# The FFN's causal convolution: three taps out of PSUM on ScalarE and two two-tile sums on VectorE, where one tap was on ScalarE and four were on VectorE

## The chip, the cores and the metric

The kernel runs on one core of a Trainium2 chip. The metric is the device time of one execution in microseconds. The engines spoken of are TensorE (PE; its weight loads are PEld), VectorE (DVE), ScalarE (ACT) and GpSimd (POOL). SyncE (SP) issues the weight loads. Data lies in SBUF, and products are summed in PSUM, in banks of 128 partitions x 512 fp32 numbers.

## What is computed

One layer of a decoder on 256 tokens of width 2048: RMSNorm, a combined input projection, a gated linear recurrence and a dilated attention, their merge, then a convolutional FFN and a last RMSNorm. The change is in the FFN alone:

```python
h = h + conv_ffn(rmsnorm(h, norm2_g), w_up, conv_w, conv_b, w_down)

def conv_ffn(u, w_up, conv_w, conv_b, w_down):
    hup = u @ w_up                               # 256 x 11264
    hc = causal depthwise conv of width 3 over the tokens (hup, conv_w) + conv_b
    a, b = hc[..., :5632], hc[..., 5632:]
    return (gelu(a) * b) @ w_down
```

Channel c of the convolution at token t is w0 x[t-2] + w1 x[t-1] + w2 x[t] + bias.

## The kernel before

All weights stream from memory as 301 units of 1 MB, each of 16 blocks of 128 x 128, through three raw buffers; SyncE issues the loads two units ahead (LOOKAHEAD). Every fp32 weight is split in two parts, a rounded one by ScalarE (L344, or L289 in two_parts) and the rest by VectorE (L345, L290), and a product takes three matmuls: L558 to L560 for the up projection, L498 to L500 for the others. The splits of a unit are written two units ahead of its matmuls, and there are six buffers for them in this stage. Every engine works through its own queue in order.

The FFN goes in 11 blocks b of 4 channel tiles for each of the two branches a and b. The up projection of a block (`sevenfold`) uses a seven-product scheme: units of a kind called S need sums of weight blocks first, made by VectorE (q at L312, raw at L314 to L317), then split as sa, se, sf and sg by L289 and L290. Its seven sums lie in seven PSUM banks; the eighth (`late_bank(8)`) belongs to the convolution.

What follows a block's up projection is the generator `hidden_side(b)`. It is advanced a step whenever a weight unit begins: `pump` gives it SIDE_US = 1.8 us a unit, and a `yield SIDE_US` spends as much, so that its instructions stand in the queues between the products of the next units. Its steps: `unfold` makes four tiles c out of the seven sums, with three accumulating DMAs by GpSimd (L582) from the scaled tiles e2, e4, e3; HIDDEN_WAIT = 3 empty steps; `convolve` for branch a (tile ua, PSUM tile ua..t), GELU over all of it (L1010); `convolve` for branch b (ub); the product g = a * g (L1016), and its split into two parts (ff) for the down projection.

`convolve` takes two halves i of two channel tiles c each. A half transposes its four 128 x 128 pieces into the one bank (L993). Then ScalarE writes the last tap and the bias of each tile (L996, Identity with a scale and a bias), and VectorE adds the other two taps, reading the bank again: L997 over 255 tokens, L998 over 254. The next half's transposes need the bank, so they wait for the last reader of this half. TensorE takes its instructions in the order of the program, so all its products behind them wait too.

After a block's up projection the down products of an earlier block follow (`DOWN`, tile dn). Each of their banks is copied by ScalarE into a staging tile dns (L1038) and added to h by an accumulating DMA of GpSimd (L1039). Staging tiles are 128 x 512; `stage` hands them out from five buffers in turn (tag o2), for unfold's t, v and e tiles and for dns. A buffer is free again when its last reader is done, which for e and dns is a DMA. The last block adds into h by VectorE (L1035).

Of the kernel before, what the change touches and what calls it, by code (L numbers as in the profile page):

```python
# [14 lines left out]
AF = mybir.ActivationFunctionType  # L15
ALU = mybir.AluOpType
# [3 lines left out]
T = 256  # L20
# [163 lines left out]
def hybrid_block(ctx, tc, x_p, x_t, weights, g1, gf, params, c_rope, c_mask0, c_mask1, c_level, out):  # L184
    nc = tc.nc
    vec, act, pe = nc.vector, nc.scalar, nc.tensor
# [13 lines left out]
    def w4(shape, name, dt=F32):  # L200
        return sb.tile([P] + list(shape), dt, tag="w4", name=name, bufs=22)

    def stage(name):
        return late["stage"].tile([P, 512], F32, tag="o2", name=name, bufs=5 if "pool" in late else STAGES - 2)
# [14 lines left out]
    def side_bank(name):  # L219
        turn[1] += 1  # L220
        return bank(4 + (turn[1] - 1) % 4, name)
# [13 lines left out]
    def pc(name, i=0):  # L235
        return par[:, POFF[name][0] + i : POFF[name][0] + i + 1]
# [419 lines left out]
    scale = float(P) ** -0.5  # L656
# [203 lines left out]
    for g in range(NGRP):  # L860
        z = four(f"z{g}", True)
        f = w4([2, HG, P], f"f{g}")
        act.activation(f, z, AF.Sigmoid)
        act.activation(z, z, AF.Sigmoid, scale=-1.0)
        for h in range(HG):
            i = g * HG + h
# [15 lines left out]
    for n in range(2):  # L882
        for j in range(NJ):
            t = w4([2, 512], f"eg{n}_{j}")
# [24 lines left out]
    for j in range(NJ):  # L909
# [7 lines left out]
        for m in range(2):  # L917
# [3 lines left out]
            pt = side_bank(f"mixt{j}_{m}")  # L921
            for c in range(4):
                pe.transpose(pt[:, c * P : (c + 1) * P], ya[:, c * P : (c + 1) * P], ident)
            pt = pt.rearrange("p (c t) -> p c t", c=4)
# [8 lines left out]
    for j in range(NJ):  # L933
        t = w4([2, 512], f"h{j}")
# [19 lines left out]
    for j in range(NJ):  # L954
# [4 lines left out]
        for i in range(2):  # L959
            pt = side_bank(f"ht{j}_{i}").rearrange("p (c t) -> p c t", c=2)  # L960
            for c in range(2):
                for m in range(2):
                    n = (2 * i + c) * P
# [15 lines left out]
    def late_bank(i, name):  # L979
        return bank(place[i], name)  # L980
# [4 lines left out]
    def convolve(ups, c0, t, name):  # L985


        for i in range(2):
            pt = late_bank(8, f"{name}t{i}").rearrange("p (c t) -> p c t", c=2)
            for c in range(2):  # L990
                for m in range(2):
                    n = (2 * i + c) * P
                    pe.transpose(pt[:, c, m * P : (m + 1) * P], ups[m][:, n : n + P], ident)  # L993
            for c in range(2):
                d, s, col = t[:, 2 * i + c], pt[:, c], c0 + 2 * i + c
                act.activation(d, s, AF.Identity, bias=pc("cb", col), scale=pc("cw2", col))  # L996
                vec.scalar_tensor_tensor(d[:, 1:], s[:, : T - 1], pc("cw1", col), d[:, 1:], op0=ALU.mult, op1=ALU.add)  # L997
                vec.scalar_tensor_tensor(d[:, 2:], s[:, : T - 2], pc("cw0", col), d[:, 2:], op0=ALU.mult, op1=ALU.add)  # L998
            yield SIDE_US

    ff = {}
# [1 line left out]
    def hidden_side(b, sums):  # L1003

        c11, c21, c12, c22 = unfold(sums, rstd2, neg2, f"up{b}")
        for _ in range(HIDDEN_WAIT - (b == 0)):
            yield SIDE_US
        a, g = (late["pool"].tile([P, FB, T], F32, tag="uc", name=f"u{n}{b}", bufs=2) for n in "ab")
        yield from convolve((c11, c21), b * FB, a, f"ua{b}")
        gelu = act.activation(a, a, AF.Gelu_apprx_tanh)  # L1010
        if b == NBLK - 1:

            with in_turn(gelu):
                act.activation(small([1], "tab", "tab", 1), eps, AF.Sqrt)
        yield from convolve((c12, c22), NFF + b * FB, g, f"ub{b}")
        vec.tensor_tensor(g, a, g, op=ALU.mult)  # L1016
        ff[b] = [w4([2, 2, T], f"ff{b}_{i}", F32R) for i in range(2)]
        for i in range(2):
            d, s = ff[b][i], g[:, 2 * i : 2 * i + 2]
            two_parts(d[:, :, 0], d[:, :, 1], s)  # L1020
# [5 lines left out]
    for b in range(NBLK):  # L1026
# [4 lines left out]
        for j, b0, b1 in DOWN.get(b, ()):  # L1031
            pst = moving(ff_parts, b0 * FB, (b1 - b0) * FB, f"dn{b}_{j}", [late_bank(i, f"dn{b}_{j}_{i}") for i in ((4, 3) if j % 2 else (1, 5))])
            for m in range(2):
                if b == NBLK - 1:
                    vec.tensor_tensor(ht[j][:, m], ht[j][:, m], pst[m], op=ALU.add)  # L1035
                else:
                    t = stage(f"dns{b}_{j}_{m}")
# [11 lines left out]
    for m in range(2):  # L1049
# [16 lines left out]
        v, r, t = v3[:, mc], r3[:, mc], s3[:, mc]  # L1066
# [57 lines left out]
```

## Time and profile before

| what | value |
|---|---|
| three runs | 1745.98, 1748.06 (median), 1751.34 us |
| profiled execution | 1748.59 us, of which the span is 1746.8 us |
| granted TensorE clock, mean | 0.997 |
| ScalarE, busy | 988.6 us, 57% |
| VectorE, busy | 1289.9 us, 74% |
| FFN stage | from about 1047 to 1738 us of the span |

The profile gives the time of each instruction in microseconds from the start of the span. A line of a timeline has the start, the duration, the engine, the line of the code, the operation, output<-inputs, the shapes and, in brackets, how long the engine sat idle before it and what ended that. Groups of instructions give the count, then the busy time in us and the mean duration in ns. Rows of waits give who waited for whom, the total, the count and the longest. The chain of waits follows the work that ended last back to what released it. Busy times of neighbours overlap a little, since an engine starts an instruction before the one before it is written out.

### The profile page before, as it was taken

Reading aid. Unit: us, or ns where it says so; the run is one execution under the profiler, and the core shown is the slowest. Engines: PE = TensorE matmul, PEld = TensorE weight load, DVE = VectorE, ACT = ScalarE, POOL = GpSimd, SP = SyncE. Lnnn points to the kernel's source line nnn. Section 1 sums busy time; section 2 is a strip of 40 time slices with the busy share of each in tenths; the row PEclk is TensorE's granted clock in tenths of the full one; section 3 lists DMA queues with packets and bytes.
Section 4 is the critical chain, followed back from the end, with each engine's and each line's share of the span. In section 5 each row is a group of like instructions: output and inputs, shape, how many; then the busy total and the mean of one; then the engine's idle time right before and its main releaser. Section 6 shows DMA issues by size and latency. Waiting matters only on the chain.

```text
span 1746.8 us, 21528 instructions
## 1 busy us (share of the span) xinstructions
PE 1726.3 (99%) x8352; PEld 1442.7 (83%) x8352; DVE 1289.9 (74%) x1610; ACT 988.6 (57%) x1253; POOL 70.1 (4%) x94
## 2 busy tenths in 40 slices
PE   9999999999999999999999999999999999999998
PEld 7888888888888888888888887788878888788886
DVE  7665575776858675444656679789988988888977
ACT  6444465555455555444445567676666666566663
POOL 0000000000000000000000000110010010010000
PEclk9999999999999999999999999999999999999999
DMA  7665644444444444556455556676677676676672
GB/s 277 230 208 199 230 145 145 170 167 172 166 169 169 169 170 168 193 193 241 178 186 190 188 189 216 194 232 228 200 235 238 190 237 235 190 235 231 198 259 97
DMA packets 58310, 346.13 MB, mean 198 GB/s; under 512 B 6704, under 2 KB 6960, under 8 KB 20064
## 3 DMA queue, kind: packets, MB, share of 16 engines
q1 hardware_dynamic: 45504, 318.02, 50.9%
q0 software_dynamic: 11408, 23.34, 6.7%
q10 hardware_dynamic: 1296, 3.41, 0.5%
q8 instruction: 65, 1.06, 0.2%
q14 instruction: 37, 0.30, 0.0%
HBM read 321.41 MB, written 2.10 MB: 185 GB/s over the span
## 4 chain that ended last, share of the span: by engine, by line
PE 90%; DMA 4%; DVE 3%; issue 1%; ACT 1%; SPq 0%; DVEq 0%; ACTq 0%
PE up L558 8%; PE up L559 8%; PE up L560 8%; DMA raw<-weights 4%; PE egp L500 3%; PE egp L498 3%; PE egp L499 3%; PE dn L498 3%; PE dn L500 3%; PE dn L499 3%; PE ak L411 3%; PE aq L411 2%; PE gp L498 2%; PE wo L498 2%; PE wo L500 2%; PE gp L500 2%
## 5 line engine op out<-in xcount | busy, mean ns | idle before, releaser
L345 DVE TENSOR_TENSOR hl<-raw,hl 128x1024 fp32r<-128x1024 f32 (+1 forms) x518 | 628.7, 1219 | 317.7 <-ACT hl L344 316.5
L344 ACT ACTIVATE hl<-raw 128x1024 fp32r<-128x1024 f32 (+1 forms) x518 | 543.2, 1054 | 536.8 <-PE egp L500 79.4
L498 PE MATMUL dn<-hl,ff 128*128 128x512 f32 x320 | 126.1, 394 | 0.0
L499 PE MATMUL dn<-hl,ff 128*128 128x512 f32 x320 | 124.8, 390 | 0.0
L500 PE MATMUL dn<-hl,ff 128*128 128x512 f32 x320 | 124.5, 390 | 0.0
L558 PE MATMUL up<-hl,hva 128*128 128x512 f32 x264 | 104.1, 394 | 0.0
L559 PE MATMUL up<-hl,hva 128*128 128x512 f32 x264 | 103.7, 393 | 0.0
L560 PE MATMUL up<-hl,hva 128*128 128x512 f32 x264 | 103.7, 393 | 0.0
L498 PE MATMUL egp<-hl,xu 128*128 128x512 f32 x256 | 100.5, 393 | 0.0
L500 PE MATMUL egp<-hl,xu 128*128 128x512 f32 x256 | 99.8, 390 | 0.0
L499 PE MATMUL egp<-hl,xu 128*128 128x512 f32 x256 | 99.7, 389 | 0.0
L500 PEld LDWEIGHTS dn<-hl,ff 128*128 128x128 f32 x320 | 60.1, 188 | 12.7
L498 PEld LDWEIGHTS dn<-hl,ff 128*128 128x128 f32 x320 | 60.1, 188 | 12.1
L499 PEld LDWEIGHTS dn<-hl,ff 128*128 128x128 f32 x320 | 60.1, 188 | 12.0
L411 PE MATMUL ak<-xu,hl 128*128 128x512 f32 x192 | 68.0, 399 | 0.0
L290 DVE TENSOR_TENSOR sa<-raw,sa 128x1024 fp32r<-128x1024 f32 x40 | 48.9, 1222 | 18.3 <-ACT sa L289 18.2
L558 PEld LDWEIGHTS up<-hl,hva 128*128 128x128 f32 x264 | 50.1, 190 | 10.7 <-ACT up0e L581 0.4
L560 PEld LDWEIGHTS up<-hl,hva 128*128 128x128 f32 x264 | 50.1, 190 | 10.5
L559 PEld LDWEIGHTS up<-hl,hva 128*128 128x128 f32 x264 | 50.1, 190 | 10.3
L500 PEld LDWEIGHTS egp<-hl,xu 128*128 128x128 f32 x256 | 48.0, 188 | 10.0
L289 ACT ACTIVATE sa<-raw 128x1024 fp32r<-128x1024 f32 x40 | 42.3, 1057 | 24.6 <-PE up L560 8.9
L499 PEld LDWEIGHTS egp<-hl,xu 128*128 128x128 f32 x256 | 48.1, 188 | 9.8
(575 smaller groups left out, 4198.7 us busy)
## 6 DMA issues: line engine op xcount, KB each, us to landing
raw<-weights SPq DMA_DIRECT2D x298, 1024.0 KB, 4.8
h<-dns POOLq DMA_DIRECT2D x36, 256.0 KB, 7.5
h<-x_t ACTq DMA_DIRECT2D x4, 512.0 KB, 5.1
xt<-x_p SPq DMA_DIRECT2D x3, 512.0 KB, 10.2
xs_q<-aqraw POOLq DMA_DIRECT2D x6, 256.0 KB, 6.9
xs_k<-akraw POOLq DMA_DIRECT2D x6, 256.0 KB, 7.2
raw<-weights SPq DMA_DIRECT2D x2, 512.0 KB, 6.6
gfb<-gf POOLq DMA_DIRECT2D x2, 512.0 KB, 13.6
```

What stands on the lines that cost most here:

```text
L289: act.activation(hi, src, AF.Copy)
L290: vec.tensor_tensor(lo, src, hi.bitcast(F32), op=ALU.subtract)
L344: last[0] = act.activation(hi[:, q * w : (q + 1) * w], raw, AF.Copy)
L345: last[1] = vec.tensor_tensor(lo[:, q * w : (q + 1) * w], raw, hi[:, q * w : (q + 1) * w].bitcast(F32), op=ALU.subtract)
L411: pe.matmul(ps, hi, pair, start=(k == 0), stop=False, skip_group_check=True)
L498: pe.matmul(pst[m], xl, hi, start=(k == k0), stop=False)
L499: pe.matmul(pst[m], xh, hi, start=False, stop=False)
L500: pe.matmul(pst[m], xh, lo, start=False, stop=(k == k0 + nk - 1))
L558: pe.matmul(sums[b], xl, wh, start=b in fresh, stop=False)
L559: pe.matmul(sums[b], xh, wh, start=False, stop=False)
L560: pe.matmul(sums[b], xh, wl, start=False, stop=left[b] == 0)
```

## The change

All three taps of a tile are now read out of the bank by ScalarE: the last one with the bias as before (Identity, now L999), and the two others with Copy and the weight as scale (L1001), into two staging tiles e, one for each tap, with room for both channel tiles of the half. VectorE then adds them from SBUF, in one tensor_tensor per tap over both tiles at once (L1003: 128x2x254 for w0's, 128x2x255 for w1's). The bank's readers are now ScalarE's alone. Each half needs two staging tiles that it didn't need before, out of the same five buffers.

```diff
@@ -991,11 +991,16 @@
                 for m in range(2):
                     n = (2 * i + c) * P
                     pe.transpose(pt[:, c, m * P : (m + 1) * P], ups[m][:, n : n + P], ident)
+
+            taps = [stage(f"{name}e{n}{i}").rearrange("p (c t) -> p c t", c=2) for n in range(2)]
+            d = t[:, 2 * i : 2 * i + 2]
             for c in range(2):
-                d, s, col = t[:, 2 * i + c], pt[:, c], c0 + 2 * i + c
-                act.activation(d, s, AF.Identity, bias=pc("cb", col), scale=pc("cw2", col))
-                vec.scalar_tensor_tensor(d[:, 1:], s[:, : T - 1], pc("cw1", col), d[:, 1:], op0=ALU.mult, op1=ALU.add)
-                vec.scalar_tensor_tensor(d[:, 2:], s[:, : T - 2], pc("cw0", col), d[:, 2:], op0=ALU.mult, op1=ALU.add)
+                col = c0 + 2 * i + c
+                act.activation(d[:, c], pt[:, c], AF.Identity, bias=pc("cb", col), scale=pc("cw2", col))
+                for n, e in enumerate(taps):
+                    act.activation(e[:, c], pt[:, c], AF.Copy, scale=pc(f"cw{n}", col))
+            for n, e in enumerate(taps):
+                vec.tensor_tensor(d[:, :, 2 - n :], d[:, :, 2 - n :], e[:, :, : T - 2 + n], op=ALU.add)
             yield SIDE_US
 
     ff = {}
```

Per half, ScalarE goes from 2 to 6 instructions and VectorE from 4 to 2. Over the program, VectorE's rows go from 1584 to 1496, ScalarE's from 1224 to 1400, and TensorE's stay at 7885. In the changed kernel, GELU is L1015, the product L1021 and the copy into dns L1043.

The order of work around the convolution moves too. VectorE in block 1, where the two halves of ua meet (ua1t0 and ua1t1 are their PSUM tiles, 190 the unit whose weights are summed in q). Before:

```order
L290 TENSOR_TENSOR se188_8483<-raw188_8437,se188_8483 128x1024
L997 SCALAR_TENSOR_TENSOR ua1_8495<-ua1t0_8497,par_85,ua1_8495 128x255
L312 TENSOR_TENSOR q190_8575<-raw190_8538 128x512
L998 SCALAR_TENSOR_TENSOR ua1_8495<-ua1t0_8497,par_85,ua1_8495 128x254
L314 TENSOR_TENSOR raw190_8538<-raw190_8538 128x512
L290 TENSOR_TENSOR sf188_8487<-raw188_8437,sf188_8487 128x1024
L997 SCALAR_TENSOR_TENSOR ua1_8495<-ua1t0_8497,par_85,ua1_8495 128x255
L998 SCALAR_TENSOR_TENSOR ua1_8495<-ua1t0_8497,par_85,ua1_8495 128x254
L345 TENSOR_TENSOR hl189_0_8532<-raw189_8493,hl189_0_8532 128x1024
L997 SCALAR_TENSOR_TENSOR ua1_8495<-ua1t1_8540,par_85,ua1_8495 128x255
L998 SCALAR_TENSOR_TENSOR ua1_8495<-ua1t1_8540,par_85,ua1_8495 128x254
```

and now (ua1e00 and ua1e10 are the staging tiles of w0's and w1's taps for half 0, ua1e01 and ua1e11 those of half 1):

```order
L290 TENSOR_TENSOR se188_8499<-raw188_8453,se188_8499 128x1024
L312 TENSOR_TENSOR q190_8599<-raw190_8558 128x512
L314 TENSOR_TENSOR raw190_8558<-raw190_8558 128x512
L1003 TENSOR_TENSOR ua1_8511<-ua1_8511,ua1e00_8518 128x2x254
L290 TENSOR_TENSOR sf188_8503<-raw188_8453,sf188_8503 128x1024
L1003 TENSOR_TENSOR ua1_8511<-ua1_8511,ua1e10_8519 128x2x255
L345 TENSOR_TENSOR hl189_0_8552<-raw189_8509,hl189_0_8552 128x1024
L1003 TENSOR_TENSOR ua1_8511<-ua1_8511,ua1e01_8565 128x2x254
L1003 TENSOR_TENSOR ua1_8511<-ua1_8511,ua1e11_8566 128x2x255
L345 TENSOR_TENSOR hl189_1_8555<-raw189_8509,hl189_1_8555 128x1024
```

Four taps out of PSUM around q and the split sf have become two sums out of SBUF, and all four sums of ua1 now stand behind q.

ScalarE in block 4, from the copies of the down products to the convolution of ub. Before:

```order
L1038 ACTIVATE dns4_3_1_9977<-dn4_3_3_9874 128x512
L289 ACTIVATE sa222_9989<-raw222_9937 128x1024
L1010 ACTIVATE ua4_9894<-ua4_9894 128x1024
L289 ACTIVATE se222_9994<-raw222_9937 128x1024
L996 ACTIVATE ub4_9895<-ub4t0_10007,par_85 128x256
L344 ACTIVATE hl223_0_10039<-raw223_10004 128x1024
L289 ACTIVATE sf222_9998<-raw222_9937 128x1024
L289 ACTIVATE sg222_10001<-q222_9987 128x512
L344 ACTIVATE hl223_1_10042<-raw223_10004 128x1024
L996 ACTIVATE ub4_9895<-ub4t0_10007,par_85 128x256
L289 ACTIVATE sa224_10084<-raw224_10045 128x1024
L289 ACTIVATE se224_10089<-raw224_10045 128x1024
```

and now:

```order
L1015 ACTIVATE ua4_9958<-ua4_9958 128x1024
L1043 ACTIVATE dns4_3_0_10046<-dn4_3_4_9937 128x512
L1043 ACTIVATE dns4_3_1_10049<-dn4_3_3_9938 128x512
L289 ACTIVATE sa222_10061<-raw222_10005 128x1024
L999 ACTIVATE ub4_9959<-ub4t0_10079,par_85 128x256
L289 ACTIVATE se222_10066<-raw222_10005 128x1024
L1001 ACTIVATE ub4e00_10084<-ub4t0_10079,par_85 128x256
L1001 ACTIVATE ub4e10_10085<-ub4t0_10079,par_85 128x256
L999 ACTIVATE ub4_9959<-ub4t0_10079,par_85 128x256
L1001 ACTIVATE ub4e00_10084<-ub4t0_10079,par_85 128x256
L1001 ACTIVATE ub4e10_10085<-ub4t0_10079,par_85 128x256
L344 ACTIVATE hl223_0_10115<-raw223_10076 128x1024
```

GELU stands ahead of the copies now, and all six taps of ub's first half stand ahead of the splits hl223_0 and sf222; the first tap is behind sa222, the others behind se222.

TensorE in block 4, at the transposes of ub's second half (ub4t1). Before:

```order
L560 MATMUL up5_2_9981<-sa222_9989,hvs2_7336 128x512
L558 MATMUL up5_7_9986<-se222_9994,hvx2_7337 128x512
L559 MATMUL up5_7_9986<-se222_9994,hvx2_7337 128x512
L993 MATMUL ub4t1_10047<-ident_87,up4c12_9784 128x128
L993 MATMUL ub4t1_10047<-ident_87,up4c22_9785 128x128
L993 MATMUL ub4t1_10047<-ident_87,up4c12_9784 128x128
```

and now:

```order
L558 MATMUL up5_5_10056<-sg220_9953,hvx0_7161 128x512
L559 MATMUL up5_5_10056<-sg220_9953,hvx0_7161 128x512
L560 MATMUL up5_5_10056<-sg220_9953,hvx0_7161 128x512
L993 MATMUL ub4t1_10123<-ident_87,up4c12_9848 128x128
L993 MATMUL ub4t1_10123<-ident_87,up4c22_9849 128x128
L993 MATMUL ub4t1_10123<-ident_87,up4c12_9848 128x128
```

They have moved from the last summed products of unit 222 ahead to those of unit 220. Between the transposes of ub's first half and these stood 49 matmuls, and now 21; from ua's first half to its second it was 30 and is 24, and from ua's second to ub's first 22 and is 24. The units and their loads stay in the same order.

## The prediction

> **What bounds the kernel now.** I read the page's head first, for who is busy.
>
> ```profile
> span 1746.8 us, 21528 instructions
> PE 1726.3 (99%) x8352; PEld 1442.7 (83%) x8352; DVE 1289.9 (74%) x1610; ACT 988.6 (57%) x1253; POOL 70.1 (4%) x94
> ```
>
> TensorE is busy for all but 20.5 us of the span. The change leaves its instructions alone, so a gain can only be idle time of TensorE, or work that it does at a low clock. The busy time that VectorE sheds and ScalarE takes on counts only through that. Second I read whom TensorE waits for; the columns are the total, the count and the longest, in us.
>
> ```profile
> PE ua1t L993 <- DVE ua L998: 3.4, 1, 3.4
> PE ua7t L993 <- DVE ua L998: 2.4, 1, 2.4
> PE ua0t L993 <- DMA up0c<-up0e: 1.2, 1, 1.2
> PE ua2t L993 <- DVE ua L998: 1.1, 1, 1.1
> PE ua4t L993 <- DVE ua L998: 0.7, 1, 0.7
> PE ua7t L993 <- DMA up7c<-up7e: 0.5, 1, 0.5
> PE ua9t L993 <- DVE ua L998: 0.2, 1, 0.2
> PE ub4t L993 <- DVE ua L998: 0.2, 1, 0.2
> ```
>
> The convolution's transposes (L993) wait for VectorE's last tap (L998): a half of a block can't be transposed into the single bank while the half before it is still being read. These rows make 3.4 + 2.4 + 1.1 + 0.7 + 0.2 + 0.2 = 8.0 us. The two DMA rows wait for the bank's input. Third, the chain through the longest of them (start, duration, what):
>
> ```profile
> 1107.20 8.40 DMA raw<-weights
> ...
> 1115.63 0.69 DVE q L312
> 1116.32 0.39 DVE ua L998
> 1116.72 0.60 DVE raw L314
> 1117.32 1.14 DVE sf L290
> ...
> 1118.88 0.49 DVE ua L998
> ...
> 1119.51 1.09 PE ua1t L993 x4
> ...
> 1124.43 0.43 PE up L558
> ```
>
> VectorE is not slow here. A weight DMA of 8.40 us lands late, the operand sum q (L312) waits for it, and the last taps stand behind q in VectorE's queue; TensorE stands behind the taps. Then the matmuls come every 0.43 us, in place of the 0.23 that the last row below shows, and the windows of the stall, the time after it and the time after that (us, then the busy time of PE, PEld, DVE, ACT and POOL, clock, DMA share, GB/s) say why:
>
> ```profile
> 1115.00:1119.50 4.50, 1.06 (x5) 0.58 (x4) 3.83 (x7) 1.51 (x2) 0.00 (x0) 0.87 0.53 88
> 1119.50:1125.10 5.60, 5.59 (x16) 4.54 (x17) 2.72 (x4) 2.07 (x3) 0.00 (x0) 0.50 0.47 178
> 1125.10:1130.00 4.90, 4.90 (x25) 4.07 (x24) 3.26 (x6) 3.05 (x4) 0.00 (x0) 1.00 0.53 214
> ```
>
> The granted clock is 0.50 for 5.6 us behind the stall. Eleven matmuls at 0.43 instead of 0.23 cost 2.2 us, and four transposes in 1.09 instead of the usual 0.63 us cost 0.5: the stall's true price is 3.4 + 2.7 us. The Trainium skill (TensorE: Matmul & The Clock Gate, Why this matters for your kernels) says that TensorE falls to half clock after an idle gap of over about 3 us; by that rule the 3.4 us stall pays twice, the 2.4 us one not, and the trace agrees: 0.50 behind the first, full pace behind the second, below.
>
> ```profile
> 1494.61 0.63 PE L993 MATMUL ua7t<-ident,up7c 128*128 128x128 f32 x4 [2.36 <-DVE ua L998]
> 1495.23 0.23 PE dn L498
> ```
>
> **VectorE's part.** Durations, of one L997, of the nearest two-tile sum (512 columns a row, from SBUF), and of the exact form of the new taps, a Copy of 128x256 out of PSUM with a pointer as scale, alone and as a pair:
>
> ```profile
> 1111.57 0.48 DVE L997 SCALAR_TENSOR_TENSOR ua<-ua1t,par,ua 128x255 f32<-128x255 f32 x1
> L290 DVE TENSOR_TENSOR ff<-ub,ff 128x512 fp32r<-128x512 f32 x22 | 14.2, 687 | 0.5 <-ACT ff L289 0.5
> L967 ACT ACTIVATE hg<-ht,par 128x256 f32<-128x256 f32 x16 | 6.7, 467 | 1.9 <-PE ht L964 1.9
> 942.82 0.84 ACT L967 ACTIVATE hg<-ht,par 128x256 f32<-128x256 f32 x2 [0.46 <-PE ht L964]
> ```
>
> There are 44 halves (11 blocks, two branches, two halves). VectorE goes per half from 4 x 0.48 = 1.92 us to 2 x 0.69 = 1.38, so it sheds 44 x 0.54 = 24 us. None of it is on the path by itself. What counts is that VectorE no longer reads the bank: all six L993 rows above that name it, 8.0 us, lose their cause, and with the long one goes the 2.7 us of low clock. I put -10.7 us, with 0 as the other end if something else is as late.
>
> **What is late next, in block 1.** The DMA that came late feeds q, and the first split of that unit (sa) comes much later:
>
> ```profile
> 1128.05 1.23 DVE L290 TENSOR_TENSOR sa<-raw,sa 128x1024 fp32r<-128x1024 f32 x1 [1.57 <-ACT sa L289]
> ```
>
> It starts 12.4 us after the landing at 1115.6 and waits for ScalarE. If TensorE runs 6.1 us earlier, 6.3 us are left, so the DMA is not next. But the adds (L1003) stand behind q as the taps did, and GELU behind the adds, and the next branch's taps behind GELU on ScalarE. From 1115.6, VectorE needs q, raw, an add, sf, an add, a split and two adds: 0.6 + 0.6 + 0.6 + 1.1 + 0.6 + 1.1 + 1.3 = 5.9, to 1121.5. GELU is then 1.05 us, six taps and two splits 4.4, to 1127. The transposes that wait for them are due at 1115.9 + 24 matmuls + 0.6 + 21 or 22 matmuls + 0.6 = 1127.5 or so. That is about even; I put +1.0 us here (0 to 2).
>
> **ScalarE's part.** Each half gains four L1001 of 0.47 us, 0.37 when they follow each other: 1.5 to 1.9 us, 66 to 82 us in all. The block is where that has to fit:
>
> ```profile
> 1288.00:1312.00 24.00, 23.08 (x108) 18.64 (x107) 19.85 (x28) 16.02 (x21) 3.53 (x4) 1.00 0.70 192
> 1301.60 0.23 PE dn L500
> 1301.18 1.28 ACT L1038 ACTIVATE dns<-dn 128x512 f32<-128x512 f32 x2 [0.19 <-PE dn L500]
> 1302.36 1.05 ACT L289 ACTIVATE sa<-raw 128x1024 fp32r<-128x1024 f32 x1
> 1303.31 1.05 ACT L1010 ACTIVATE ua<-ua 128x1024 f32<-128x1024 f32 x1
> 1302.97 0.63 PE L993 MATMUL ub4t<-ident,up4c 128*128 128x128 f32 x4 [0.23 <-DVE ua L998]
> 1314.59 0.61 PE L993 MATMUL ub4t<-ident,up4c 128*128 128x128 f32 x4
> ```
>
> ScalarE works 16.0 of these 24 us; four halves' new taps add 6 to 7.5, and it would work 22 to 23.5, that is 92 to 98%. And the second half of ub, now 11.6 us and 49 matmuls behind the first, moves to 21 matmuls behind it: 0.6 + 21 x 0.23 = 5.4 us. The order on ScalarE is then: two staging copies, sa, the first tap, se, five taps. Copies start 0.4 us before the last down matmul does (1301.60 less 1301.18, the chain's row and the copies') and give way to sa after 1.18 us; sa and se hold 0.95 each, the six taps some 0.40: done 5.1 us after that matmul's start. The transposes come 0.2 + 5.4 = 5.6 us after it. The margin is 0.4 to 0.5 us, for ua by the same count 0.8. A wait of 0 to 0.6 us for ub in each of the seven blocks 3 to 9 is what these hold; I take 0.2 x 7 = 1.4, since a negative margin takes a split more than the order has, and keep 0 and 4.2.
>
> The five staging buffers are taken by two taps a half too, so a tap waits until the accumulating DMA of an older dns has landed:
>
> ```profile
> DMA to landing us min/median/max: 3.3/7.5/11.0
> ```
>
> The third dns of a block must land for the last tap of ub's second half, some 7 us after its issue: about 1 us of hold at the median, 4 at the longest. Behind it in ScalarE's queue stand splits, whose lead decides whether that counts:
>
> ```profile
> 1283.00:1350.00 67.00, 66.08 (x300) 54.15 (x299) 59.40 (x75) 43.98 (x56) 6.14 (x7) 1.00 0.73 228
> 1299.48 1.06 ACT L344 ACTIVATE hl<-raw 128x1024 fp32r<-128x1024 f32 x1 [1.15 <-PE dn L500]
> 1462.95 1.23 DVE L290 TENSOR_TENSOR sf<-raw,sf 128x1024 fp32r<-128x1024 f32 x1
> 1465.70 0.39 PE L558 MATMUL up<-sf,hvx 128*128 128x512 f32 x1
> ```
>
> The first row is a whole block, windows as above: ScalarE is idle for 23 of 67 us. In the convolution's stretch it waits for TensorE to free the buffers of a split (1.15 us), so it has lead, and I price the hold at nothing. The cover is thinnest at the last summed unit of a block: split done at 1464.18, used at 1465.70, 1.5 us. The waits for c (1.2 + 0.5) stay.
>
> **Sum.** 1748.6 (span and 1.8 around it) - 8.0 - 2.7 + 1.0 + 1.4 = 1740.3. The profiled execution is 0.5 above the median of the runs: 1739.8, said as 1740.
>
> **Rivals.** *No measurable change, 0.27.* The waits change their owner. One more split (0.95) ahead of the taps than I count, and each of blocks 1 to 9 loses 0.55 at ub and 0.15 at ua: 6.3, with 2 in block 1: 1737.9 + 8.3 = 1746, less 0.5. For it: margins of 0.4 and 0.8 us and a nearly full ScalarE. Against: a split ahead of the taps is one less behind them, and only the place in the queue shifts.
>
> *Slower, 0.12.* ScalarE becomes the bound of each block: held by the staging slots and by 7.5 us more work per block (four halves of 1.9), it falls behind with the splits, past the 1.5 us of lead at the last summed unit. If 3.4 us of lag are left there, ten blocks lose 1.9 us each: 1737.9 + 19 = 1757. It decides from a lag of 1.5 us, and pays from 2.6 (ten times 1.07 eats the 10.7). Against it: of the block's 23 idle us, 15 would be left after the 7.5, and the last summed unit lies at the block's end, far behind the convolution. The Trainium skill (ScalarE: Activation LUTs, Rules for kernel authors) says to do adds and multiplications on VectorE, not on ScalarE. By that rule the taps' scaling is in the wrong place, and this rival is what it would cost; the trace bears it out only weakly, with 467 ns for a tap on ScalarE against 480 on VectorE.
>
> *The stall returns at another door, in the forecast's share.* If block 1 still stops TensorE for over 3 us, the 2.7 us stay too: 1740.3 + 2.7 + 2.4 = 1745, near the first rival. That the change doesn't free the bank from VectorE is excluded by its lines.
>
> **How the numbers follow.** A measurement of this kernel tells about 0.3%, 5.2 us, from no change: faster is below 1742.8, slower above 1753.3. The forecast has 0.61; the first rival 0.27, the second 0.12. The range reaches from 1736 (the floor of 1737.9 less the 2 us by which the lowest run lies under the median) to 1749, which takes in the first rival and the scatter of the runs, and leaves out the second. The signed chances are faster 0.6, same 0.28, slower 0.12, for the forecast's upper edge touches 1742.8.
>
> **What would show it.** Right: no L993 row that names VectorE, clock 1.00 from 1115 to 1125, VectorE about 24 us less busy, ScalarE 66 to 82 more, L993 waits for ScalarE of 1 to 4 us in all. Wrong: L993 waits for ScalarE of 6 us or more; matmuls (L498, L558) that wait for a split; a window at clock 0.50.

## The result and the profile after

The changed kernel takes 1740.04 us (median of five runs, 1737.84 to 1740.83), against 1748.06 us before. The ratio is 0.9947, with a 95% interval of 0.9929 to 0.9965: about 8 us faster. Its profiled execution took 1740.42 us, with a span of 1738.6.

The head of the page first:

```profile
span 1738.6 us, 21613 instructions
PE 1723.5 (99%) x8352; PEld 1442.6 (83%) x8352; DVE 1271.5 (73%) x1522; ACT 1045.4 (60%) x1429; POOL 70.1 (4%) x94
```

VectorE is 18.4 us less busy and ScalarE 56.8 us more. TensorE's busy time fell by 2.8 us although it does the same work. 1.0 of that lies ahead of block 0's transposes; of the rest, 1.1 is low clock, which cost 2.7 us behind the old stall and 1.6 behind the new one below. Whom TensorE waits for, all rows of the FFN stage (total, count, longest):

```profile
PE ub1t L993 <- ACT ub1e L1001: 2.3, 1, 2.3
PE ua0t L993 <- DMA up0c<-up0e: 1.6, 1, 1.6
...
PE ua2t L993 <- ACT ua2e L1001: 0.5, 1, 0.5
```

No transposes wait for VectorE any more: six rows and 8.0 us are gone. In their place stand two rows with ScalarE, 2.8 us. The same three windows around block 1's old stall, and one more (us, busy time of PE, PEld, DVE, ACT and POOL, clock, DMA share, GB/s):

```profile
1115.00:1119.50 4.50, 4.50 (x22) 3.67 (x21) 4.04 (x6) 3.73 (x8) 0.00 (x0) 1.00 0.20 36
1119.50:1125.10 5.60, 5.60 (x28) 4.64 (x27) 4.52 (x6) 3.36 (x6) 0.00 (x0) 1.00 0.75 236
1125.10:1130.00 4.90, 2.62 (x11) 1.89 (x11) 4.87 (x7) 4.90 (x9) 0.00 (x0) 0.87 0.38 159
...
1129.00:1131.00 2.00, 2.00 (x6) 1.51 (x6) 2.00 (x4) 2.00 (x6) 0.00 (x0) 0.50 0.35 57
```

The old stall and its half clock are gone. A new stall sits 8.5 us later (1128.05 for 1119.51), and the half clock stands behind that one. Its making, in one row each of VectorE, ScalarE and TensorE (start, duration, and in brackets the idle time before and what ended it):

```profile
1115.42 0.69 DVE L312 TENSOR_TENSOR q<-raw 128x512 f32<-128x512 f32 x1 [4.26 <-DMA raw<-weights]
1121.74 1.06 ACT L1015 ACTIVATE ua<-ua 128x1024 f32<-128x1024 f32 x1 [2.51 <-DVE ua L1003]
1128.05 0.66 PE L993 MATMUL ub1t<-ident,up1c 128*128 128x128 f32 x4 [2.27 <-ACT ub1e L1001]
```

The weight DMA is as late as before. The sums stand behind q, GELU waits 2.51 us for the sums, ub's taps stand behind GELU on ScalarE, and ub's second transposes wait for the taps.

Where the time went is best seen block by block: from the first L993 of a block's ua to that of the next, in us, worked out from the starts of those rows in each profile. 64.5 is a block in which nothing waits.

| from block | before | after |
|---|---|---|
| 1 | 60.7 | 58.6 |
| 2 | 54.9 | 54.6 |
| 3 | 64.7 | 64.5 |
| 4 | 65.7 | 64.6 |
| 7 | 67.9 | 64.6 |
| 9 | 65.0 | 64.6 |

Block 7 gives 3.3 us, block 1 gives 2.1 and block 4 gives 1.1. Another 0.6 is there already when block 0's transposes begin, at 1057.53 in place of 1058.17. That lies ahead of everything that the change touches, and in the profiles of all the kernels here this start lies anywhere from 1057.53 to 1059.36, so I count it as no part of the change. The remaining 1.1 of the 8.2 us comes in tenths.

### The profile page after: what moved, and what is told of

The parts are those of the page before. It is cut to its first block, busy times and chain, and to the rows that moved or that the text cites. A ratio compares the mean times of both kernels' runs of the same rounds, so it can differ in the third digit from the quotient of the medians.

```text
span 1738.6 us, 21613 instructions
## 1 busy us (share of the span) xinstructions
PE 1723.5 (99%) x8352; PEld 1442.6 (83%) x8352; DVE 1271.5 (73%) x1522; ACT 1045.4 (60%) x1429; POOL 70.1 (4%) x94
## 4 chain that ended last, share of the span: by engine, by line
PE 92%; DMA 3%; DVE 2%; ACT 1%; issue 1%; SPq 0%; POOL 0%; DVEq 0%; ACTq 0%; POOLq 0%
PE up L560 8%; PE up L558 8%; PE up L559 8%; PE dn L498 3%; PE dn L500 3%; PE dn L499 3%; PE egp L498 3%; PE egp L500 3%; PE egp L499 3%; PE ak L411 3%; DMA raw<-weights 2%; PE aq L411 2%; PE gp L498 2%; PE wo L498 2%; PE wo L500 2%; PE gp L500 2%
## 5 line engine op out<-in xcount | busy, mean ns | idle before, releaser
L499 PEld LDWEIGHTS dn<-hl,ff 128*128 128x128 f32 x320 | 60.2, 188 | 11.9
L289 ACT ACTIVATE se<-raw 128x1024 fp32r<-128x1024 f32 x40 | 42.5, 1061 | 25.6 <-DVE raw L314 17.1
```

The costliest lines, as they stand in the source:

```text
L289: act.activation(hi, src, AF.Copy)
L499: pe.matmul(pst[m], xh, hi, start=False, stop=False)
```

## The experiments

The theory: the gain is that the bank no longer hangs on VectorE's queue, in which late work stands ahead of the taps. The rivals: the gain is VectorE's lighter load, or it comes from the new order of the transposes. Each kernel below was timed together with the kernel before, and the ratio is to that. The rows and heads of a kernel come from one profiled execution of it.

**Four sums a half in place of two** (e1). One part of the change is undone:

```diff
-            for n, e in enumerate(taps):
-                vec.tensor_tensor(d[:, :, 2 - n :], d[:, :, 2 - n :], e[:, :, : T - 2 + n], op=ALU.add)
+            for c in range(2):
+                for n, e in enumerate(taps):
+                    vec.tensor_tensor(d[:, c, 2 - n :], d[:, c, 2 - n :], e[:, c, : T - 2 + n], op=ALU.add)
```

> The changed kernel, but VectorE adds each tap of each tile by itself: four sums a half in place of two, all from SBUF; ScalarE alone reads the bank, as in the changed kernel. Theory (the bank: what was gained is that the transposes no longer stand behind VectorE's queue): as the changed kernel, 1738 to 1743 us, no L993 row that names VectorE. Rival (the load: what was gained is VectorE's lighter queue): with four instructions a half again most of the gain is lost, 1745 to 1749.

Measured: 1739.75 us, ratio 0.9948 (0.9934 to 0.9962). The two-tile sum adds nothing to the gain. As a test of the load it is weak, for VectorE's busy time is only 3.9 us above that of the changed kernel, as this head shows:

```profile
PE 1723.1 (99%) x8352; PEld 1443.0 (83%) x8352; DVE 1275.4 (73%) x1610; ACT 1044.7 (60%) x1429; POOL 70.2 (4%) x94
```

**ScalarE copies the bank, VectorE keeps its four taps** (e2):

```diff
-            taps = [stage(f"{name}e{n}{i}").rearrange("p (c t) -> p c t", c=2) for n in range(2)]
...
+            e = stage(f"{name}e{i}").rearrange("p (c t) -> p c t", c=2)
+            act.activation(e, pt, AF.Copy)
+            for c in range(2):
+                d, s, col = t[:, 2 * i + c], e[:, c], c0 + 2 * i + c
+                act.activation(d, pt[:, c], AF.Identity, bias=pc("cb", col), scale=pc("cw2", col))
+                vec.scalar_tensor_tensor(d[:, 1:], s[:, : T - 1], pc("cw1", col), d[:, 1:], op0=ALU.mult, op1=ALU.add)
+                vec.scalar_tensor_tensor(d[:, 2:], s[:, : T - 2], pc("cw0", col), d[:, 2:], op0=ALU.mult, op1=ALU.add)
```

> ScalarE copies the bank whole, both tiles in one instruction, into one staging tile, and writes the last tap from the bank; VectorE keeps all its four scalar_tensor_tensor a half, now reading the copy. So VectorE's work is that of before and only the bank is freed by ScalarE, with three instructions a half in place of six. Theory (the bank): the whole gain, and less of the new wait at ub1t: 1737 to 1741. Rival (the load): no gain, 1745 to 1750.

Measured: 1738.83 us (1735.12 to 1743.23), ratio 0.9943 (0.9927 to 0.9959). Its head:

```profile
span 1733.3 us, 21551 instructions
PE 1720.8 (99%) x8352; PEld 1443.4 (83%) x8352; DVE 1284.4 (74%) x1610; ACT 1005.3 (58%) x1297; POOL 70.1 (4%) x94
```

VectorE does the same taps as before, 5.5 us less busy in all, and by the median the gain is whole. The rival of the load falls here. This profile is of the fastest of the six runs. In it no L993 row with ScalarE or VectorE is left: with three ScalarE instructions a half in place of six, the bank's readers in block 1's ub are done at 1124.75 even behind GELU, and its second transposes run at 1125.35.

**The kernel before without the middle tap** (e3): w1's part of the convolution is left out of the result.

```diff
-                vec.scalar_tensor_tensor(d[:, 1:], s[:, : T - 1], pc("cw1", col), d[:, 1:], op0=ALU.mult, op1=ALU.add)
```

> The kernel before without the middle tap: w1's product and sum are left out, so VectorE has two instructions a half and is about 42 us less busy, more than the change takes from it; VectorE still reads the bank last, and in block 1 its tap still stands behind q. Theory (the bank): ua1t still waits some 3 us for VectorE with a low clock behind it, ua7t 1.5 to 2.5; 1744 to 1749. Rival (the load): at least the change's gain, 1740 or less.

Measured: 1747.74 us, ratio 0.9989 (0.9978 to 1.0). Its head, and the row of TensorE's waits that matters (its L997 is the other tap):

```profile
PE 1726.2 (99%) x8352; PEld 1443.3 (83%) x8352; DVE 1252.7 (72%) x1522; ACT 989.8 (57%) x1253; POOL 70.1 (4%) x94
...
PE ua1t L993 <- DVE ua L997: 2.3, 1, 2.3
```

VectorE is 37 us less busy than before, twice what the change takes from it, and by the median almost nothing is gained. In the profiled execution ua1's wait was shorter than the 3 us I expected, with a half clock behind it, and block 7's was gone; of VectorE's other waits 0.7 us at ua8 was left. That execution (1744.53) lies near the low end of the twelve runs, 1742.65 to 1751.07. From block 0's first transposes on it took 5.1 us less than the profile before, so there these waits were shorter, be it by the load or by the order; the median doesn't keep it.

**One tap moved** (e4): w1's tap goes to ScalarE and a two-tile sum, w0's stays on VectorE and reads the bank.

```diff
...
+                act.activation(e[:, c], pt[:, c], AF.Copy, scale=pc("cw1", col))
...
+            vec.tensor_tensor(d[:, :, 1:], d[:, :, 1:], e[:, :, : T - 1], op=ALU.add)
+            for c in range(2):
+                col = c0 + 2 * i + c
+                vec.scalar_tensor_tensor(d[:, c, 2:], pt[:, c, : T - 2], pc("cw0", col), d[:, c, 2:], op0=ALU.mult, op1=ALU.add)
```

> Half of the change: ScalarE takes w1's tap into a staging tile and VectorE adds it for both tiles at once; w0's tap stays on VectorE and reads the bank. Theory (the bank): the bank still hangs on VectorE behind q, so ua1t waits 3 us or more; 1744 to 1751. Rival (the load): about half of the gain, 1743 to 1745.

Measured: 1749.72 us, ratio 1.0003 (0.9991 to 1.0015). TensorE's waits for VectorE's tap (L1004), the largest four:

```profile
PE ua1t L993 <- DVE ua L1004: 3.0, 1, 3.0
PE ua9t L993 <- DVE ua L1004: 1.5, 1, 1.5
...
PE ua7t L993 <- DVE ua L1004: 1.3, 1, 1.3
...
PE ua4t L993 <- DVE ua L1004: 1.1, 1, 1.1
```

Half of the change is worth nothing: with one reader of the bank left in VectorE's queue, 7.3 us of these waits stay. The transposes have a new order here too: ub's are 28 matmuls apart in block 4, and 25 in e3, in place of 49. So a new order by itself doesn't bring the gain. The changed kernel's own order (24, 24 and 21 matmuls apart; e1, e2, e6 and e7 have it too) was never run with a reader left on VectorE, so for blocks 4 and 7 reader and order aren't parted to the end. But that order has ua's halves 24 matmuls apart in place of 30, which leaves the bank's readers less time, not more.

**q behind the taps, before otherwise unchanged** (e5). The sum that waits for the late DMA is issued behind the last L998 that the program has emitted by then (tap):

```diff
-        vec.tensor_tensor(q1, r[:, 0], r[:, 3], op=ALU.add)
+        with in_turn(*tap):
+            vec.tensor_tensor(q1, r[:, 0], r[:, 3], op=ALU.add)
...
```

> The kernel before with one thing moved: the sum q of a weight unit (the one that waits for the late weight DMA) is issued on VectorE behind the convolution's taps that the program has by then, so in block 1 behind all eight taps of ua1. The taps stay on VectorE and read the bank, VectorE's work is unchanged, and the transposes keep about their old places (31, 20 and 39 matmuls apart in block 1). Theory (the bank behind VectorE's queue, and the queue behind the late DMA): no wait of ua1t for VectorE over 1 us and no low clock there, 1738 to 1744. Rival (only taking the taps off VectorE's PSUM reads helps, or the new order of the transposes does): 1746 to 1750.

Measured: 1745.93 us, ratio 0.998 (0.9964 to 0.9995): a miss of 2 us on the theory's range and, at 1745.93, just under the rival's. The waits of the FFN stage (its lines are two further down):

```profile
PE ua1t L995 <- DMA up1c<-up1e: 3.4, 1, 3.4
...
PE ua5t L995 <- DVE ua L1000: 0.2, 1, 0.2
```

The transposes' waits for VectorE did go, from 8.0 to 0.2 us, but the order around unfold moved too. Two of the accumulating DMAs of block 1 were issued at 1107.51 in place of 1100.54, and now ua1's first transposes wait for them, with a low clock behind. The edit traded one stall for another and didn't settle the matter, so I made it narrower.

**q behind the taps for one unit only** (e9): the same edit for unit 190 alone, the one in block 1.

```diff
-        with in_turn(*tap):
+        with in_turn(*(tap if u == 190 else ())):
```

> As the kernel with q moved, but only for the one sum that stood in the way in block 1 (q of unit 190): VectorE does it behind all eight taps of ua1, and everything ahead of it stays as before, so the input of ua1's transposes comes no later than before. Theory (the bank behind VectorE's queue, and the queue behind the late DMA): block 1, from its first transposes to block 2's, takes 54 to 57 us in place of 60.7, and blocks 4 and 7 stay as before, with their waits for VectorE: 1741 to 1745 in all. Rival (the stall in block 1 has another cause than q's place): 59 us or more, 1746 to 1750.

Measured: 1744.81 us (1740.93 to 1747.81), ratio 0.9975 (0.9964 to 0.9986). VectorE's rows in block 1, with the last taps of both halves ahead of q, ua1's second transposes, and TensorE's waits for VectorE that are left (lines are two further down, as in e5):

```profile
1115.69 0.48 DVE L1000 SCALAR_TENSOR_TENSOR ua<-ua1t,par,ua 128x254 f32<-128x254 f32 x1
...
1121.67 0.48 DVE L1000 SCALAR_TENSOR_TENSOR ua<-ua1t,par,ua 128x254 f32<-128x254 f32 x1
1122.07 0.68 DVE L314 TENSOR_TENSOR q<-raw 128x512 f32<-128x512 f32 x1
...
1116.37 0.60 PE L995 MATMUL ua1t<-ident,up1c 128*128 128x128 f32 x4
```

```profile
PE ua2t L995 <- DVE ua L1000: 1.8, 1, 1.8
...
PE ua4t L995 <- DVE ua L1000: 1.4, 1, 1.4
...
PE ua3t L995 <- DVE ua L1000: 0.7, 1, 0.7
PE ua7t L995 <- DVE ua L1000: 0.5, 1, 0.5
```

Block 1 takes 54.5 us in place of 60.7, by the starts 1109.54 and 1164.01 of its and block 2's first transposes. The weight DMA was no earlier: it landed at 1116.2, in place of 1115.6, and ua's second transposes still ran at 1116.37, without a wait. The other blocks keep waits for VectorE, as expected, though of other sizes than before (1.8 us in block 2 for 1.1, 0.5 in block 7 for 2.4). All taps are on VectorE and read the bank; only the late sum left their way. That shows the cause of block 1's stall: the late DMA, by way of q, in the queue on which the bank hangs. It also shows that q has time: begun 6.4 us later than before (1115.63), nothing behind it in block 1 is late.

**GELU late** (e6), on the changed kernel; tap is here the last L1001 emitted:

```diff
...
-        gelu = act.activation(a, a, AF.Gelu_apprx_tanh)
...
         yield from convolve((c12, c22), NFF + b * FB, g, f"ub{b}")
+        with in_turn(tap[0]):
+            gelu = act.activation(a, a, AF.Gelu_apprx_tanh)
```

> The changed kernel with GELU of a block issued on ScalarE behind the last tap of ub, in place of between ua and ub. Theory (what is left of a wait at ub1t is ScalarE held by GELU, which waits for the sums behind q): the 2.3 us at ub1t and the low clock behind it go, 1735 to 1738.5. Rival (the wait is ScalarE's own work, the splits between the taps): it stays at 1.5 us or more, 1739.5 to 1741.

Measured: 1737.53 us (1736.44 to 1737.87), ratio 0.9928 (0.9912 to 0.9945). The waits of the FFN stage (lines are one further down), then ub1's two sets of transposes and, on ScalarE, the first split behind GELU's old place:

```profile
PE ua0t L994 <- DMA up0c<-up0e: 2.0, 1, 2.0
...
PE ua2t L994 <- ACT ua2e L1002: 0.3, 1, 0.3
```

```profile
1122.42 0.60 PE L994 MATMUL ub1t<-ident,up1c 128*128 128x128 f32 x4
...
1128.00 0.66 PE L994 MATMUL ub1t<-ident,up1c 128*128 128x128 f32 x4
...
1122.62 1.06 ACT L290 ACTIVATE sa<-raw 128x1024 fp32r<-128x1024 f32 x1 [1.52 <-PE up L561]
```

The row of ub1t is gone. But this profile doesn't show by itself that it was GELU's hold. The taps were done at 1127.95, as late as in the changed kernel (1128.00); what differs is that TensorE came to ub1's first transposes 2.3 us later, at 1122.42 for 1120.14, after a longer wait and a half clock in block 0. A TensorE that late would have met next to nothing of a stall of 2.27 us even with GELU in its old place. What speaks for GELU is an estimate: the split sa now waits for TensorE and not behind GELU, so with a TensorE 2.3 us earlier it would start near 1120.3, and the taps would end near 1125.7, about when the transposes are due (1125.8). The times agree with that: the median lies 2.5 us under that of the changed kernel, and four of the six runs lie under that kernel's fastest, 1737.84, the other two 0.03 above it; but the intervals of the two ratios overlap.

**The copy and GELU late** (e7): e2 with GELU moved as in e6, where tap is the last L999 emitted.

```diff
-                act.activation(d, pt[:, c], AF.Identity, bias=pc("cb", col), scale=pc("cw2", col))
+                tap[:] = [act.activation(d, pt[:, c], AF.Identity, bias=pc("cb", col), scale=pc("cw2", col))]
...
+        with in_turn(tap[0]):
+            gelu = act.activation(a, a, AF.Gelu_apprx_tanh)
```

> The kernel with the whole-bank copy (three ScalarE instructions a half, VectorE's four reading the copy), with GELU late as well. Theory: the copy alone already had no wait of L993 for ScalarE in its profile, so GELU's place is worth little there: 1737 to 1739.5. Rival (GELU's hold costs in most runs, and the profile of the copy was a lucky one): 1734 to 1736.

Measured: 1736.3 us (1735.38 to 1738.69), ratio 0.9925 (0.9907 to 0.9942). It has the lowest median of all, but against e6 and e2 the intervals overlap, so which of the three is best isn't settled. It sits between the two expectations' ranges, in neither; what the late GELU adds to the copy, 2.5 us by the medians, is within the scatter of the copy's runs.

**ScalarE's taps twice** (e8), on the changed kernel:

```diff
-                    act.activation(e[:, c], pt[:, c], AF.Copy, scale=pc(f"cw{n}", col))
+                    for _ in range(2):
+                        act.activation(e[:, c], pt[:, c], AF.Copy, scale=pc(f"cw{n}", col))
```

> The changed kernel with each L1001 issued twice (the second writes the same numbers again): four more ScalarE instructions of some 0.4 us a half, 44 x 4 x 0.4 = 70 us more work for ScalarE. The order of the program gives the transposes more room for it (32, 27 and 51 matmuls apart in block 4, where the changed kernel has 24, 24 and 21). Theory (ScalarE has room outside the transposes' waits): 1739 to 1746. Rival (ScalarE is near its bound in a block, the slower case of the prediction): 1753 or more, with matmuls that wait for splits.

Measured: 1749.75 us, ratio 1.0004 (0.999 to 1.0017). Between the two ranges, so neither theory had the size. Its head and its waits:

```profile
PE 1729.6 (99%) x8352; PEld 1441.8 (82%) x8352; DVE 1269.8 (73%) x1522; ACT 1110.3 (63%) x1605; POOL 70.2 (4%) x94
...
PE dn L498 <- DVE ff L290: 3.8, 1, 3.8
PE ua5t L993 <- DMA up5c<-up5e: 1.4, 1, 1.4
...
PE ua7t L993 <- DMA up7c<-up7e: 1.3, 1, 1.3
PE ua4t L993 <- DMA up4c<-up4e: 1.1, 1, 1.1
```

65 us more work for ScalarE cost 9.7 us, the whole gain. This profile is of one of the slowest of the twelve runs (1752.28; the range is 1746.83 to 1752.68). Nothing waits at the bank for the taps, and no row names a split of weights. What comes late by these rows is the split of ff for the down product, 3.8 us once, and unfold's accumulating DMAs, which land after the transposes are due, 1.1 to 1.4 us in these blocks. For ff the trace shows the way: from 1087.6 until ff's split at 1100.18 ScalarE has no idle time of over 0.15 us, with the doubled taps among its splits; ub's last sum and the product follow the taps, and the split starts when the product ends. For the DMAs it doesn't: in block 5 ScalarE idles 1.33 us for a weight DMA 3 us before it writes e, so why they land late is open. The order of the program is another one here too, and the 9.7 us are the price of both.

## Why the prediction was right

The time came out as forecast: 1740.04 against 1740.0. The mechanism stands, but that the number fits so closely is in part luck. Block 1 cost 2.9 us more than its term, and a wait at ua2, for which the sum had nothing, cost 0.5; ub cost 1.4 less than its term, a DMA wait in block 7 fell by 0.5, and 1.4 us that no term had fell too: 0.6 ahead of the change and 0.8 in tenths.

- *The waits for VectorE, -8.0.* Right: all six rows are gone, and e2 against e3 shows that VectorE's load doesn't decide. That the bank's reader in VectorE's queue does, e9 shows for block 1; for blocks 4 and 7 it rests on e4 and e9, where a reader stays there and so do waits, and on the changed kernel, e1 and e2, where neither does. Blocks 4 and 7, whose waits no new one replaced, got 1.1 and 3.3 us faster for the 0.9 and 2.4 us of the rows (block 7 also lost a DMA wait of 0.5).
- *The low clock behind the long stall, -2.7.* Right for that stall, but a low clock came back behind the new one. Eight matmuls at 0.43 us in place of 0.23 cost 1.6 us. The sum had no such term; only the rival of the stall at another door had one, with a limit of 3 us that the new stall of 2.27 us undercuts. The prediction named a window at clock 0.50 as a sign of being wrong, and one is there, behind another stall than the one it priced.
- *Block 1, +1.0.* This is the term that failed in size. It measured 2.3 of wait and 1.6 of low clock, 3.9, outside its bounds of 0 to 2. The path was right at its middle (sums done at 1121.7, forecast 1121.5), and the taps were done at 1128.0, forecast 1127. The mistake was in the step "due at 1115.9 + 24 matmuls": 1115.9 is where ua's second transposes stood before, 30 matmuls behind the first. The order puts 24 there now, and they ran at 1114.15. So TensorE came to ub's second transposes at 1125.8, not 1127.5. The taps were 1.0 us later than forecast because of a third split: sa, se and sf stood among them, where the count had two. This one stood ahead of the last tap:

```profile
1126.56 1.07 ACT L289 ACTIVATE sf<-raw 128x1024 fp32r<-128x1024 f32 x1
```

So in block 1 the first rival's one more split did come.
- *ub in blocks 3 to 9, +1.4.* Measured 0, within its bounds, but nearer to a cost than I said. The end of the taps and the transposes in block 4:

```profile
1302.01 0.86 ACT L1001 ACTIVATE ub4e<-ub4t,par 128x256 f32<-128x256 f32 x2
...
1302.93 0.66 PE L993 MATMUL ub4t<-ident,up4c 128*128 128x128 f32 x4
```

The taps end at 1302.87, and the transposes start at 1302.93: a margin of 0.06 us, where I had 0.4 to 0.5. In e1 the same place waits 0.6 us in block 3 and 0.3 in block 5. The first rival needed only one more split there.
- *The staging buffers, nothing.* Nearly right. In block 1 no transposes waited for such a hold (first row below). In block 2 a tap of ua's first half was held for 0.38 us, the half's taps ended at 1172.49, and ua's second transposes waited 0.45 for them: that is the row of ua2, and most of it goes back to the buffers.

```profile
ACT ua1e L1001 <- DMA h<-dns: 1.3, 2, 0.8
...
1170.83 0.47 ACT L1001 ACTIVATE ua2e<-ua2t,par 128x256 f32<-128x256 f32 x1 [0.38 <-DMA h<-dns]
...
1172.54 0.66 PE L993 MATMUL ua2t<-ident,up2c 128*128 128x128 f32 x4 [0.45 <-ACT ua2e L1001]
```

- *Busy times.* The durations were nearly right (a two-tile sum 684 ns on average, forecast 690; a tap 490, forecast 470), but VectorE shed 18.4 us and not 24, and ScalarE gained 56.8 and not 66 to 82. I added durations; the busy time counts neighbours that overlap only once. The durations of VectorE's taps and sums alone do make 84.2 us before and 60.2 now, 24.0 less.
- *The slower rival.* It didn't come. e8 shows that its direction was sound, but with other victims: with 65 us more on ScalarE, ff and unfold's DMAs were late, and not the last summed unit. The Trainium skill (ScalarE: Activation LUTs, Rules for kernel authors) would have the taps' products on VectorE. The trace didn't bear that out even weakly, as the prediction had it: 467 ns for a tap on ScalarE is less than 480 on VectorE. Here that rule didn't decide, since the bank's release was worth more than 56.8 us of an engine that had them; e2 does both, with the products on VectorE and only a copy on ScalarE, and is no slower.

With the sum mended (-8.0 - 2.7 + 3.9 + 0.5 for ua2, and -0.5 for the DMA wait in block 7) the change is worth 6.8 us from block 0's first transposes on. The span fell by 7.6 there, and by 0.6 ahead of them. The last 0.8 us are spread over the blocks in tenths, and I can name no wait for them.

## What to carry to other kernels

When a tensor engine waits for a buffer, ask which queue its last reader stands in and what else stands there, and move the reader out of the queue that can be held, not merely some of the load: with one reader left behind (e4), 7.3 of the 8.0 us stayed. A copy that frees the buffer can be enough. Then follow the held work to the next queue (here the sums, GELU, and the taps behind GELU), and count the margins from the places that the new order gives, not from the old times.

## What the runs showed of the hardware

The clock fell behind shorter gaps than I had assumed. The 2.27 us stall shown above brought 0.50, like e3's at ua1t with 2.34, e6's wait at ua0t with 2.03 and e5's there with 1.94, while 2.36 us in block 7 of the kernel before didn't, nor 1.50 (e3, e4) or 1.76 us (e9, ua2t). So in these traces the length of a wait alone doesn't decide between 1.9 and 2.4 us. The Trainium skill (TensorE: Matmul & The Clock Gate, Why this matters for your kernels) sets the limit at about 3 us, and these four shorter waits differ from it. In e5's window behind the 3.4 us wait the clock was as low as behind the first stall, and for as long:

```profile
1116.00:1122.00 6.00, 6.00 (x17) 4.80 (x18) 2.23 (x4) 1.04 (x2) 0.00 (x0) 0.52 1.05 286
```
